# One early product in another bank, and a seventh product ahead of a fourth, in a hybrid attention trunk

## The chip, the cores and the metric

The kernel runs on one core of one Trainium2 chip. The metric is the device time of one execution in microseconds (us). Each profiled execution comes with its own time and with the span of its instructions. The engines are named as in the profile: PE multiplies matrices, PEld loads its weights, DVE and ACT work elementwise (both read what PE left in its accumulators), POOL is a third elementwise engine, and SP issues most of the transfers.

## The reference

One decoder layer over 1024 positions of width 1024 in float32. A normed input is projected to 7184 columns, which feed eight heads of differential softmax attention and four heads of chunked gated linear attention. Both results are normed and gated, and one output projection follows.

```python
h = rms_norm(x, pre_g)
z = jnp.einsum('bsd,de->bse', h, w_in)
qa, ka, va, ga, qb, kb, vb, gb, gk_low = split_columns(z)
...
oa = diff_attention(qa, ka, va, lam)        # softmax(q1 k1) - lam * softmax(q2 k2), times v
gk = jnp.einsum('bsr,re->bse', gk_low, w_gk_up) + b_gk
ob = gla_chunked(qb, kb, vb, log_sigmoid(gk) / 16)
y = jnp.einsum('bse,ed->bsd', jnp.concatenate([oa, ob], axis=-1), w_out)
return x + rms_norm(y, post_g)
```

(Reshapes, norms and gates of the two branches are left out.)

## The kernel before

**The input projection by Strassen's seven products.** For each block of 256 columns, a "pair" p, `w_in` is cut in two halves of rows and two halves of columns, and `h` likewise, and seven products n = 1 to 7 stand for eight. `LEFT` names the block of `h` of each (h11, h12, s1 to s4, h22); each block is kept as a high and a low part, and each product is three passes: high by high, high by low, low by high. Product 1 leaves its sum in a PSUM bank x and a copy s1 of it (`snap`, L427, on ACT); product 6 adds to the same bank and is copied as s2; product 7 adds again and is copied as s3. Product 2 takes a bank y of its own, 5 a bank z, 4 a bank y, and 3 adds to z. Each output quarter (`done`) is the sum, on DVE, of a bank and a copy. For value columns ("VB", "VA") it is L403, for others L440.

**Banks.** There are eight PSUM banks. `take_bank` takes the first number of the list `free`, and whoever is through with a bank appends it. The list is worked in the order in which the program is written; on the chip, a matmul into a bank waits until the last reader of the bank is done.

**The start.** The 1024 rows of x are normed and transposed on PE (`xT`, L120) in two halves. `first(0)` and `first(1)` make h11 and h12. Then `blocks(j)`, j = 0 to 3, each transposes two tiles of the second half into two banks, from which ACT and DVE make h22 and the blocks s1, s2, s3 (L522, L562, L565, L568, L569 and L547/L548). Between these, `go(1)` runs one early product. `step(i)` runs product i of the list `order`; its first ten entries are written out by hand, and the products of the first group (pairs 0 and 1, the first value columns) and of the second (pairs 2 and 3) follow, so that products 5, 6, 4, 7, 3 of the first group come as (0,5) (1,5) (0,6) (1,6) (0,4) (0,7) (1,4) (1,7), with (0,3) (1,3) later. The swap of (1,4) and (0,7) is written out:

```python
i = order.index((1, 4))
order[i : i + 2] = order[i + 1], order[i]
```

With each product, `make_weights` prepares the weights three products ahead: a difference on DVE (L296), a rounded copy on ACT (L315) and the rest on DVE (L316), in a ring of five slots. A wide group (two pairs) uses two slots for a product.

**The low-rank step.** After `go(6)`, `low_rank()` (L630 to L677) loads a 1024 x 16 slice of `w_in` (tile wd) and makes of it a padded matrix wl on DVE (L647, L649 twice, L650 twice) and, of another small input, ku (L653 to L656). It then runs `go(2)`, which is the two last products (1,4) and (1,7) of the first group, and then the product `gkl_ps`, which multiplies by wl.

**After that** come the other pairs, the linear attention, from about 640 us on the scores of the softmax attention (`sc`, in three banks; DVE reads them at L1039, ACT takes the exponential at L1049, POOL and DVE combine the two maps at L1055 and L1058, PE transposes the result, `wtr`), and the output projection.

**Order of work.** PE's order is the program's. The order of DVE, ACT and SP is drawn up at build time by a list scheduler that plans with costs of its own, so a change at one place can reorder these queues at others. Each engine works its queue strictly in order.

Of the kernel before, what the change touches and what calls it, by code (L numbers as in the profile page):

```python
# [19 lines left out]
HB = 4  # L20
# [11 lines left out]
def hymba_kernel(  # L32
# [75 lines left out]
    free = list(range(8))  # L108

    def take_bank(shape, name):  # L110
        i = free.pop(0)
        return bank(i, shape, name), i
# [6 lines left out]
    def tr(dst, src):  # L119
        tc.keep_in_program_order(pe.transpose(dst, src, ident))  # L120
# [11 lines left out]
    def block(n):  # L132
        if n not in H:
            pool_h, pieces = (hpool, 1) if n in ("s3", "s4") else (hw, 2)
            H[n] = [
                [
                    pool_h.tile(
                        [P, HB // pieces, 512], F32R, tag=f"{n}_{part}{i}", name=f"{n}_{part}"
                    )
                    for i in range(pieces)  # L140
                ]
                for part in ("hi", "lo")
            ]
        return H[n]
# [12 lines left out]
    def t2k(tag, bufs, name, dt=F32, shape=(P, 512)):  # L157
        return ap.tile(list(shape), dt, tag=tag, name=name, bufs=bufs)

    def t_c(name, dt=F32):  # L160
        return t2k("c", 4, name, dt)
# [19 lines left out]
    def wide(p):  # L181
        return pairs[p][0] in ("VA", "VB")
# [17 lines left out]
    order = [(0, 1), (1, 1), (0, 2), (1, 2), (2, 1), (3, 1), (2, 2), (3, 2), (4, 1), (4, 2)]  # L200
    n_early = len(order)
    y, z = len(pairs) - 2, len(pairs) - 1
# [12 lines left out]
                order += [(p, 3) for p in prev]  # L215

    i = order.index((1, 4))
    order[i : i + 2] = order[i + 1], order[i]

    order += [(y, 1), (y, 2), (y - 1, 3), (y, 5), (z, 1), (z, 2), (z, 5), (y, 6), (z, 6), (y, 4)]  # L220
    order += [(y, 7), (z, 4), (z, 7), (y, 3), (z, 3)]
# [16 lines left out]
    def prepare(i):  # L238

        if i >= len(order) or i in ws:  # L240
            return
        if i < 4:

            act_ins, dve_ins = normed[0][:2]
            with tc.issue_after(act_ins.ins), tc.issue_after(dve_ins.ins):
                make_weights(i)
        else:
            make_weights(i)
# [73 lines left out]
    def multiply(i, ps, start):  # L322
        p, n = order[i]
        hi, lo = H[LEFT[n]]
        w = ws.pop(i)
        if not wide(p):
            for j, (a, b) in enumerate(((0, hi), (1, hi), (0, lo))):
                for k in range(HB):
                    mm(
                        ps, w[a][:, k, :], at(b, k),  # L330
                        start=(start and j == 0 and k == 0), stop=(j == 2 and k == HB - 1),
                        skip_group_check=not start,
                    )
            return

        for j, (a, b) in enumerate(((0, hi), (1, hi), (0, lo))):
            for k in range(HB):
                for t in range(2):
                    c = (p % 2 * 2 + t) * P
                    mm(  # L340
                        ps[:, t * 256 : t * 256 + 256], at(b, k)[:, c : c + P], w[a][:, k, :],
                        start=(start and j == 0 and k == 0 and t == 0),
                        stop=(j == 2 and k == HB - 1), skip_group_check=True,
                    )
# [51 lines left out]
    def take_values(p, half, unit, p0, p1):  # L396

        kind, n, _ = pairs[p - p % 2]
        tiles = slice(half * 4 + p % 2 * 2, half * 4 + p % 2 * 2 + 2)
        p0, p1 = (t.rearrange("p (n u c) -> p u n c", u=2, c=P) for t in (p0, p1))  # L400
        if kind == "VB":
            st = t_st("gv_st").rearrange("p (u n c) -> p u n c", u=2, c=P)
            dve.tensor_tensor(st, p0, p1, ALU.add)  # L403
            for u in range(2):
                sp.dma_start(gv_d[n + unit][u, :, tiles, :], st[:, u])
        else:
            c, hi = t_c("c"), t_st("v_hi", F32R)
            c, hi, lo = (
                t.rearrange("p (u n c) -> p u n c", u=2, c=P) for t in (c, hi, c.bitcast(F32R))
            )  # L410
            dve.tensor_tensor(c, p0, p1, ALU.add)
            act.copy(hi, c)
            dve.tensor_tensor(lo, c, fp(hi), ALU.subtract)
            for t, src in enumerate((hi, lo)):
                for u in range(2):
                    sp.dma_start(v_d[n + 2 * unit + u][t, :, tiles, :], fp(src[:, u]))
# [3 lines left out]
    def step(i):  # L420

        p, n = order[i]
        kind, m, _ = pairs[p]
        def snap(k, ps):
            other = k == "s3" and (wide(p) or p >= len(pairs) - 2)
            b[k] = t_c("s") if other else t2k("s", 4, "s")
            act.copy(b[k], ps)  # L427

        b = sums.setdefault(p, {})
        name = {1: "x", 2: "y", 5: "z", 6: "x", 4: "y", 7: "x", 3: "z"}[n]  # L430
        if n in (1, 2, 4, 5):
            b[name], b["i" + name] = take_bank([P, 512], name)
        ps = b[name]
        multiply(i, ps, n not in (6, 7, 3))

        def done(half, unit, p0, p1):
            if wide(p):
                return take_values(p, half, unit, p0, p1)
            c = t_c("c")
            dve.tensor_tensor(c, p0, p1, ALU.add)  # L440
            take(kind, m, half, unit, c)

        if n == 1:
            snap("s1", ps)
        elif n == 2:
            done(0, 0, ps, b["s1"])
            free.append(b["iy"])
        elif n == 6:
            snap("s2", ps)
        elif n == 7:  # L450
            snap("s3", ps)
            free.append(b["ix"])
            done(1, 1, b["z"], b["s3"])
            done(1, 0, b["y"], b["s3"])
            free.append(b["iy"])
        elif n == 3:
            done(0, 1, ps, b["s2"])
            free.append(b["iz"])
# [60 lines left out]
    def put(ps, k, dst, j):  # L519
        hi, lo = dst  # L520
        act.activation(at(hi, j), ps, AF.Copy, scale=pre_g[:, k : k + 1])
        dve.scalar_tensor_tensor(  # L522
            at(lo, j), ps, pre_g[:, k : k + 1], fp(at(hi, j)), ALU.mult, ALU.subtract
        )
# [20 lines left out]
    def parts(n, j, f):  # L545
        hi, lo = block(n)
        act.copy(at(hi, j), f)  # L547
        dve.tensor_tensor(at(lo, j), f, fp(at(hi, j)), ALU.subtract)  # L548

    def blocks(j):  # L550


        pss = []
        for k in (j, j + HB):
            ps, i = take_bank([P, 512], "xT")
            for n in range(4):
                tr(ps[:, n * P : (n + 1) * P], xs[4 + n][:, k * P : (k + 1) * P])
            pss.append(ps)
            free.append(i)
        k = j + HB  # L560
        h21 = t_c("h21")
        act.activation(h21, pss[0], AF.Copy, scale=pre_g[:, j : j + 1])  # L562
        put(pss[1], k, block("h22"), j)
        s1 = t_c("s1")
        dve.scalar_tensor_tensor(s1, pss[1], pre_g[:, k : k + 1], h21, ALU.mult, ALU.add)  # L565
        parts("s1", j, s1)
        h11 = f1[0][:, j]
        dve.tensor_tensor(h21, h11, h21, ALU.subtract)  # L568
        dve.tensor_tensor(h11, s1, h11, ALU.subtract)  # L569
        parts("s2", j, h11)  # L570
        parts("s3", j, h21)
# [8 lines left out]
    def wo_step(n):  # L580
        if n in (1, 6) and wo_open:
            e, dh, raw = wo_open.pop()
            hi = t_c("wo_hi", F32R)
            act.copy(hi, raw)
            lo = raw.bitcast(F32R)
            dve.tensor_tensor(lo, raw, fp(hi), ALU.subtract)
            for t, src in enumerate((hi, lo)):
                sp.dma_start(wod[e][t][:, cols(dh)], fp(src))
        if n in (2, 4) and wo_todo:
            e, dh = wo_todo.pop(0)  # L590
            raw = ap.tile([P, 512], F32, tag="t4", name="wo_raw", bufs=1)
            sp.dma_start(raw, w_out[0, e * P : (e + 1) * P, cols(dh)])
            wo_open.append((e, dh, raw))

    def go(n):
        for _ in range(n):
            i = made[0]
            if i == len(order):
                return
            made[0] = i + 1  # L600
            for a in range(4):
                prepare(i + a)
            step(i)
            if order[i][0] > EARLY and not (wide(order[i][0]) and order[i][0] % 2):
                wo_step(order[i][1])
            if fill and next(fill[0], 0) == 0:
                fill.pop(0)
# [10 lines left out]
    go(1)  # L618
    for j in range(HB):
        blocks(j)  # L620
        go(1)
    go(2)
    s4 = [kp.tile([P, 2, 512], F32, tag=f"k{i}", name="s4") for i in range(2)]
# [902 lines left out]
```

## Time and profile before

| | |
|---|---|
| three runs | 980.25, 978.34, 980.24 us; median 980.24 |
| profiled execution | 979.08 us; span of its instructions 977.4 us; TensorE clock granted 0.999 |
| PE busy | 956.7 us (98% of the span) |
| DVE / ACT / POOL busy | 735.4 / 600.5 / 142.9 us |

In a line of the timeline the first number is the start in us from the beginning of the span, the second the duration, then engine, source line, operation, tiles (written <- read), shape and count; square brackets give idle time of the engine just before and what ended it. In a table of waits, a row says which engine's instruction waited for which other: total us, times, longest. In a table of windows a row gives, after the stretch and its length, the busy time of PE, PEld, DVE, ACT and POOL, then the granted clock.

### The profile page before, as it was taken

To read this page: it belongs to the slowest core of one execution; us is meant where nothing else is said; L and a number is where in the kernel's file an instruction comes from. 1 tells how busy PE (TensorE), PEld (TensorE's weight loads), DVE (VectorE), ACT (ScalarE), POOL (GpSimd) and SP (SyncE) were. 2 spreads that over 40 slices of the span, in tenths; PEclk is the share of its full clock that TensorE was granted. 3 is DMA by queue.
4 is the path that set the end of the run, shared out by engine and by line. 5 is a ranking of instruction groups with operands and counts; after the bars stand their busy time and mean duration, and the time that the engine had idled before them with its cause. 6 is when DMAs were issued, how large, how long until landed. Compare 5 with 4: busy or idle time off the path is not lost.

```text
span 977.4 us, 15766 instructions
## 1 busy us (share of the span) xinstructions
PE 956.7 (98%) x5338; PEld 830.4 (85%) x5338; DVE 735.4 (75%) x1452; ACT 600.5 (61%) x1164; POOL 142.9 (15%) x158
## 2 busy tenths in 40 slices
PE   5999999999999999999999999999999999999997
PEld 5998988888889998999888888878888888888785
DVE  6887597789866667686786876487888888898554
ACT  8742455487357455454665775366776687887773
POOL 4300000000000010000200002121322222443321
PEclk9999999999999999999999999999999999999999
DMA  9432446656774868897987866987656669994677
GB/s 345 151 110 91 139 135 205 231 179 225 238 247 162 264 187 286 254 294 229 293 259 243 273 202 191 407 269 272 197 186 228 240 199 344 340 294 105 151 208 147
DMA packets 152593, 220.45 MB, mean 226 GB/s; under 512 B 17104, under 2 KB 83664, under 8 KB 152416
## 3 DMA queue, kind: packets, MB, share of 16 engines
q1 hardware_dynamic: 146176, 203.71, 64.1%
q0 software_dynamic: 6336, 15.73, 7.0%
q8 instruction: 42, 0.69, 0.3%
q14 instruction: 39, 0.32, 0.1%
HBM read 133.93 MB, written 88.60 MB: 228 GB/s over the span
## 4 chain that ended last, share of the span: by engine, by line
PE 95%; DVE 2%; ACT 1%; DMA 1%; issue 1%; POOL 0%; SPq 0%; DVEq 0%; ACTq 0%; POOLq 0%
PE x L117 24%; PE y L117 15%; PE z L117 15%; PE ypart L117 13%; PE sc L117 7%; PE po L117 5%; PE yps L117 4%; PE wtr L120 3%; PE gpo L117 3%; PE kv L117 1%; PE gkl_ps L117 1%; PE pa L117 1%; DMA x<-in_x_dram 1%; PE xT L120 1%; DVE s_lo L548 0%
## 5 line engine op out<-in xcount | busy, mean ns | idle before, releaser
L315 ACT CAST w<-w_raw 128x512 fp32r<-128x512 f32 (+1 forms) x164 | 112.4, 688 | 94.7 <-PE y L117 44.1
L316 DVE TENSOR_TENSOR w<-w_raw,w 128x512 fp32r<-128x512 f32 (+1 forms) x164 | 126.7, 774 | 50.1 <-ACT w L315 43.3
L1049 ACT ACTIVATE p<-p,stt 128x896 f32<-128x896 f32 (+7 forms) x128 | 99.3, 777 | 36.7 <-DVE stt L1039 33.9
L427 ACT COPY s<-x 128x512 f32<-128x512 f32 x84 | 49.1, 585 | 84.4 <-PE x L117 84.3
L775 POOL TENSOR_SCALAR_AFFINE_SELECT gan<-gan 128x512 f32<-128x512 f32 x8 | 16.5, 2060 | 485.4 <-ACT gan L774 449.8
L296 DVE TENSOR_TENSOR w_raw<-w_raw 128x512 f32<-128x512 f32 (+1 forms) x96 | 75.9, 791 | 13.9 <-DMA w_raw<-in_w_in_dram 12.6
L1039 DVE CUSTOM_DVE_ANT_0 p<-sc,maskt 128x512 f32<-128x512 f32 (+3 forms) x128 | 74.3, 585 | 14.5 <-PE sc L117 13.3
L117 PE MATMUL ypart<-wo_hi,m_hi 128*128 128x512 f32 x192 | 79.5, 414 | 0.1
L117 PE MATMUL y<-h_hi,w 128*128 128x512 f32 x320 | 79.6, 391 | 0.0
L117 PE MATMUL z<-s_hi,w 128*128 128x512 f32 x320 | 79.6, 391 | 0.0
L117 PE MATMUL x<-s_hi,w 128*128 128x512 f32 x320 | 79.6, 391 | 0.0
L1055 POOL TENSOR_SCALAR p<-p,stt,lam 128x1024 f32<-128x1024 f32 (+3 forms) x64 | 56.2, 879 | 146.9 <-DVE stt L1054 141.9
L117 PE MATMUL ypart<-wo_hi,m_lo 128*128 128x512 f32 x192 | 75.5, 393 | 0.0
L117 PE MATMUL ypart<-wo_lo,m_hi 128*128 128x512 f32 x192 | 75.4, 393 | 0.0
L117 PE MATMUL sc<-k,q 128*128 128x512 f32 (+1 forms) x192 | 69.0, 363 | 1.3 <-DVE stt L1039 1.2
L117 PEld LDWEIGHTS x<-s_hi,w 128*128 128x128 f32 x320 | 59.7, 188 | 12.2
L117 PEld LDWEIGHTS y<-h_hi,w 128*128 128x128 f32 x320 | 59.6, 188 | 12.2
L117 PEld LDWEIGHTS z<-s_hi,w 128*128 128x128 f32 x320 | 59.5, 188 | 12.0
L117 PE MATMUL sc<-ks,q 128*128 128x512 f32 (+1 forms) x192 | 66.1, 347 | 0.0
L1097 ACT CAST wt_hi<-wtr 128x512 fp32r<-128x512 f32 (+1 forms) x80 | 42.7, 534 | 24.6 <-PE wtr L120 23.8
L1098 DVE TENSOR_TENSOR wt_lo<-wtr,wt_hi 128x512 fp32r<-128x512 f32 (+1 forms) x80 | 50.7, 633 | 8.6 <-ACT wt_hi L1097 8.0
L1058 DVE SCALAR_TENSOR_TENSOR p<-p,stt,p 128x1024 f32<-128x1024 f32 (+3 forms) x64 | 52.1, 814 | 4.1 <-POOL p L1055 3.9
(226 smaller groups left out, 2247.7 us busy)
## 6 DMA issues: line engine op xcount, KB each, us to landing
w_raw<-in_w_in_dram SPq DMA_DIRECT2D x56, 512.0 KB, 4.7
wo_raw<-in_w_out_dram SPq DMA_DIRECT2D x32, 256.0 KB, 3.0
wo_d<-wo_hi SPq DMA_DIRECT2D x32, 256.0 KB, 2.8
wo_d<-wo_raw SPq DMA_DIRECT2D x32, 256.0 KB, 3.8
q<-q_d SPq DMA_DIRECT2D x32, 256.0 KB, 4.7
k<-k_d SPq DMA_DIRECT2D x32, 256.0 KB, 5.7
ks<-k_d SPq DMA_DIRECT2D x64, 128.0 KB, 6.2
v<-v_d SPq DMA_DIRECT2D x16, 512.0 KB, 7.0
```

The costliest lines, as they stand in the source:

```text
L117: tc.keep_in_program_order(pe.matmul(*a, **k))
L120: tc.keep_in_program_order(pe.transpose(dst, src, ident))
L296: dve.tensor_tensor(dst, a, b, ALU.subtract)
L315: act.copy(w[0], src)
L316: dve.tensor_tensor(w[1], src, fp(w[0]), ALU.subtract)
L427: act.copy(b[k], ps)
L1039: ins = dve.tensor_tensor_reduce(p[:, a:e], sc[:, : e - a], maskt[:, NZ + P - (e - a) :] if last else maskt[:, : e - a], 1.0, 3e38 if i == ...
L1049: act.activation(p[:, :n], p[:, :n], AF.Exp, bias=st[:, m : m + 1], scale=-1.0, accum_out=st[:, 2 + m : 3 + m],)
L1055: pool.tensor_scalar(p1[:, :n], p1[:, :n], st[:, 5:6], lam, ALU.mult, ALU.mult)
L1058: dve.scalar_tensor_tensor(p0[:, :n], p0[:, :n], st[:, 4:5], p1[:, :n], ALU.mult, ALU.subtract)
L1097: act.copy(hi[:, :n], pt[:, :n])
L1098: dve.tensor_tensor(lo[:, :n], pt[:, :n], fp(hi[:, :n]), ALU.subtract)
```

## The change

Three edits. First, the order of the first group's second half becomes (0,4) (0,7) (1,7) (1,4): product 7 of pair 1 stands ahead of its product 4. Second, since the quarter `done(1, 0)` needs bank y of product 4 and copy s3 of product 7, it is now run by whichever of the two comes last, and the bank y is given back there. Third, after the last `blocks` and ahead of the product that follows, the second entry of `free` is moved to the front. The list there is [6, 0, 2, 5] and becomes [0, 6, 2, 5]: product 2 of pair 3 takes bank 0 in place of bank 6, and product 1 of pair 4 takes 6 in place of 0. Work and shapes are the same.

```diff
     i = order.index((1, 4))
-    order[i : i + 2] = order[i + 1], order[i]
+    order[i : i + 3] = order[i + 1], order[i + 2], order[i]
...
             done(1, 1, b["z"], b["s3"])
-            done(1, 0, b["y"], b["s3"])
-            free.append(b["iy"])
+        if n in (4, 7):
+            b.setdefault("both", []).append(n)
+            if len(b["both"]) == 2:
+                done(1, 0, b["y"], b["s3"])
+                free.append(b["iy"])
         elif n == 3:
...
     for j in range(HB):
         blocks(j)
+        if j == HB - 1:
+
+            free.insert(0, free.pop(1))
         go(1)
```

## The prediction

> **What bounds the kernel now.** I read the page's first two lines, then PE's own table of waits.
>
> ```profile
> span 977.4 us, 15766 instructions
> PE 956.7 (98%) x5338; PEld 830.4 (85%) x5338; DVE 735.4 (75%) x1452; ACT 600.5 (61%) x1164; POOL 142.9 (15%) x158
> ...
> PE y L117 <- DVE s L565: 1.3, 1, 1.3
> PE sc L117 <- DVE stt L1039: 1.2, 2, 0.9
> PE y L117 <- ACT s L427: 0.7, 1, 0.7
> ```
>
> PE is busy 98% of the span, and after its start-up only some 3 us of waits are named. The change aims at the first and the third of these, 2.0 us together. So every shift of PE that is not taken back later is a shift of the end, and the questions are what PE meets next after each wait that goes, and whether a new wait appears.
>
> **First edit: the bank.** (timeline of PE and DVE, and one row of the windows)
>
> ```profile
> 41.63 1.04 PE L120 MATMUL xT<-ident,xt 128*128 128x128 f32 x8
> 43.98 2.15 PE L117 MATMUL y<-w,h_hi 128*128 128x256 f32 x16 [1.32 <-DVE s L565]
> ...
> 41.83 0.69 DVE L403 TENSOR_TENSOR gv_st<-y,s 128x512 f32<-128x512 f32 x1 [0.16 <-PE y L117]
> ...
> 42.50:62.00 19.50, 18.08 (x128) 16.79 (x127) 19.50 (x29) 10.46 (x16) 0.74 (x1) 1.00 0.21 63
> ...
> 58.09 1.22 DVE L316 TENSOR_TENSOR w<-w_raw,w 128x1024 fp32r<-128x1024 f32 x1
> 58.15 2.44 PE L117 MATMUL x<-w,s_hi 128*128 128x256 f32 x16
> 59.37 1.01 PEld L117 LDWEIGHTS x<-w,s_hi 128*128 128x128 f32 x8 [0.30 <-DVE w L316]
> ```
>
> Before, product 2 of pair 3 waits for L565 to read bank 6. With bank 0 it waits for L403, which reads product 2 of pair 2 there and ends at 41.83 + 0.69 = 42.52. The transposes ahead of it on PE end at 41.63 + 1.04 = 42.67. So it starts at about 42.6 and not at 43.98: 1.35 us gained at this place.
>
> The next product with a late operand is (0,6). Its second eight matmuls need the low weights that L316 writes from 58.09 to 59.31. PE already waited for it there: PEld 59.37 follows its end by 0.06. DVE is busy all of 42.50 to 62.00, 19.50 of 19.50 us. As built, the changed kernel's DVE queue holds the same instructions between L403 at 41.83 and this L316, in a slightly other order; none goes, and none of them waits for a PE product that comes earlier. So L316 ends at 59.31 again, and PE, which reaches it 1.35 us earlier, waits 1.35 us longer. The 1.3 us are not gained but moved; the sum takes 0. (The bounds are 0 and -1.35.) Behind that L316, the changed queue has L363 ahead of the last low part of s2, which is 0.6 us later, at 61.1; PE wants it at 59.4 + 0.96 + 0.72, so 0.1 us at most is lost.
>
> **Second edit: the order.** (timeline of PE, ACT and DVE)
>
> ```profile
> 67.15 2.08 PE L117 MATMUL x<-w,s_hi 128*128 128x256 f32 x16
> 70.87 2.18 PE L117 MATMUL y<-w,h_hi 128*128 128x256 f32 x16 [0.68 <-ACT s L427]
> 73.85 2.08 PE L117 MATMUL x<-w,s_hi 128*128 128x256 f32 x16
> 76.72 2.00 PE L117 MATMUL gkl_ps<-h_hi,wl 128*64 128x512 f32 x8
> ...
> 70.23 0.59 ACT L427 COPY s<-x 128x512 f32<-128x512 f32 x1 [1.62 <-PE x L117]
> ...
> 71.00 0.69 DVE L403 TENSOR_TENSOR gv_st<-z,s 128x512 f32<-128x512 f32 x1
> ...
> 72.20 0.40 DVE L653 CAST ku<-gk_up 16x512 fp32r<-16x512 f32 x1
> ...
> 73.08 0.23 DVE L647 TENSOR_TENSOR wd<-wd 128x64 f32<-128x64 f32 x1
> 73.23 0.22 DVE L649 CAST wl<-wd 128x128 fp32r<-128x128 f32 x1
> 73.48 0.68 DVE L655 TENSOR_TENSOR ku<-gk_up,ku 16x512 fp32r<-16x512 f32 x1
> 74.17 0.68 DVE L656 TENSOR_TENSOR ku<-gk_up,ku 16x512 fp32r<-16x512 f32 x1
> 74.89 1.22 DVE L316 TENSOR_TENSOR w<-w_raw,w 128x1024 fp32r<-128x1024 f32 x1
> 76.03 0.19 DVE L649 CAST wl<-wd 128x64 fp32r<-128x64 f32 x1
> 76.14 0.28 DVE L650 TENSOR_TENSOR wl<-wd,wl 128x128 fp32r<-128x128 f32 x1
> ...
> 77.47 1.22 DVE L296 TENSOR_TENSOR w_raw<-w_raw 128x1024 f32<-128x1024 f32 x1
> ...
> 81.26 1.23 DVE L296 TENSOR_TENSOR w_raw<-w_raw 128x1024 f32<-128x1024 f32 x1 [1.24 <-DMA w_raw<-in_w_in_dram]
> ...
> 86.95 2.08 PE L117 MATMUL z<-w,s_hi 128*128 128x256 f32 x16
> ```
>
> A product takes 76.72 - 73.85 = 2.87 us. (0,7) starts at 67.15 and so ends its issue at 70.02. Before, (1,4) takes the bank that (0,7) filled and waits for the copy at L427 (70.23 to 70.82): it starts at 70.87, 0.85 late. Now (1,7) follows, into its own bank, whose copy is long done. It starts at 70.02, (1,4) at 72.89 with its bank long copied, and PE is free for `gkl_ps` at 75.76: 0.96 us before 76.72. That is the intended gain.
>
> But `gkl_ps` needs wl, whose last part for it is L650 at 76.14 to 76.42, only 0.3 us ahead of PE before. And the changed DVE queue has three instructions newly ahead of this L650, or differently placed. From 71.00 on it reads: L403, L403, L653, L654, then L316 (which stood behind L656), L647, L649, L655, L656, then the L403 of (1,7) and a 1024-wide L296 (both stood behind L650), then L649 and L650. L403 is there because (1,7) now comes earlier. By the rows, start to start: the two L403 72.20 - 71.00 = 1.20; L653 and L654 73.08 - 72.20 = 0.88; L316 76.03 - 74.89 = 1.14; L647 0.15; L649 0.25; L655 0.69; L656 0.72; L403 half of 1.20, so 0.60; L296, as long as L316, 1.14; L649 0.11; L650 to its end 0.28. The sum is 7.16. The queue starts when the copy of (0,7) is done, about 70.9. So wl is ready at 78.06 and PE starts `gkl_ps` at about 78.1 in place of 76.72: **1.4 us lost**, a new PE wait of 2.3 us. Nothing on the way waits longer than its turn: the ring slot of this L316 is free when (1,7) is through its first sixteen matmuls, about 72.1, and its turn comes at 73.0; the copy for the L403 of (1,7) is made by 73.7, and its turn is at 75.8. DVE has no idle there that could absorb the three, and L650's cover before was 0.3 us. A pace two tenths off either way gives 1.2 and 1.6 as ends.
>
> SP's queue is moved too: the stores behind that L403 now stand ahead of one weight load, which also waits for an L316 that DVE reaches some 1.6 us later. The L296 that reads this load (81.26, after a wait of 1.24 for it) then ends near 84.1. Behind it on DVE stands the reader of the first `gkl_ps`, which frees the bank that the product at 86.95, now 88.3, takes: over 3 us of cover, so I cost it at nothing. If that cover were gone, each us of it would be a us of PE.
>
> From 76.72 to 631 us PE has no wait in the table, so the 1.4 us pass on whole: nothing there has slack to lose or to give.
>
> **Far from the edits: the first scores.** The changed queues differ once more, at 643 to 660 us, where the scheduler put DVE's L1058 (128x896) ahead of the second half of L1039, and the 640-wide L1058 behind an L1039. Times here are those of before; all engines are shifted alike.
>
> ```profile
> 643.84 1.11 POOL L1055 TENSOR_SCALAR p<-p,stt,lam 128x896 f32<-128x896 f32 x1 [3.33 <-DVE stt L1054]
> ...
> 644.94 0.48 DVE L1039 CUSTOM_DVE_ANT_0 p<-sc,maskt,stt 128x256 f32<-128x256 f32 x1
> 645.35 1.15 DVE L1058 SCALAR_TENSOR_TENSOR p<-p,stt,p 128x896 f32<-128x896 f32 x1
> 645.49 0.50 PE L117 MATMUL sc<-k,q 128*128 128x512 f32 x1
> ...
> 647.16 0.33 PE L117 MATMUL sc<-k,q 128*128 128x128 f32 x1 [0.94 <-DVE stt L1039]
> ...
> 651.31 0.89 DVE L1058 SCALAR_TENSOR_TENSOR p<-p,stt,p 128x640 f32<-128x640 f32 x1 [0.42 <-POOL p L1055]
> ...
> 652.54 0.60 PE L120 MATMUL wtr<-ident,p 128*128 128x128 f32 x4
> ```
>
> L1058 must wait for POOL, 643.84 + 1.11 = 644.95, so that half of L1039 starts 1.06 later (646.41 - 645.35 before, by L1058's pace), and the product at 645.49, into the bank that it frees, at 646.6: 1.1 late. The wait of 0.94 at 647.16 takes nearly all of this back. But the exponential of that half, and with it POOL and the later L1058, also come about 1 us later; the 640-wide L1058 starts near 652.2 and ends near 653.1, and the transposes at 652.54 that read it start 0.6 late. Nothing later on PE waits. I take **0.6 us**; its ends are 0 (the shift is eaten by the wait at 647.16) and 1.7 (both stalls count in full).
>
> [...] New PE waits of 1.7 us at 57.7 and of 2.3 us at 75.8 could cost more than themselves.
>
> ```profile
> 14.41 4.24 PE L117 MATMUL x<-w,h_hi 128*128 128x256 f32 x16 [0.58 <-ACT h_hi L521]
> 18.45 1.72 PE L117 MATMUL x<-w,h_lo 128*128 128x256 f32 x8
> ...
> 23.67 1.12 PE L117 MATMUL x<-w,h_lo 128*128 128x256 f32 x8
> ```
>
> Eight equal matmuls take 1.72 us at the start and 1.12 a little later: PE starts slow. After the 1.32 us idle at 43.98 there is no such thing (16 in 2.15). [...] No run here shows an idle of 2.3 us.
>
> **Sum.** 0 + 1.4 + 0.6 = +2.0 us. On the profiled execution, 979.08, this gives 981.1; on the median, 980.24, which is 1.2 higher, 982.2. I forecast the middle, 981.7. About 0.2% (2.0 us) is what a measurement of this kernel can tell from no change.
>
> **Rivals.**
> - **Both waits simply go** (faster). If L316 at 58.09 and wl at 76.42 came earlier with PE, the gain is 1.35 + 0.96, less 0.6: 1.7 to 2.3, so about 978. For it: these are the two waits that PE's table names. Against: DVE has no idle from 42.5 to 62 and decides both. It needs DVE to finish 1 us earlier than its rows add up to. 0.08.
> - **Only the wl wait counts**: the stall of the scores is absorbed at 647.16. +1.4, 981.1. The wait of 0.94 speaks for it. 0.07.
> - **The scores cost in full**, 1.7 in place of 0.6: +3.1, 982.8. 0.10.
> - **The clock falls** in the 2.3 us wait. The start's 24 slow matmuls end at 20.17, 5.8 us after 14.41; at the pace of 23.67 they take some 3.1. +2.6 more, 984.3. The 43.98 row speaks against it. 0.05.
>
> **How the numbers follow.** The forecast has 0.70. It lies on the border of 0.2%; since 0.1 us at 61.1 was left out of the sum I put 0.44 of it above and 0.26 within. Slower: 0.44 + 0.10 + 0.05 = 0.59. Same: 0.26 + 0.07 = 0.33. Faster: 0.08. The range runs from 979.7, the wl wait alone on the lowest run (978.34 + 1.4), to 984.0, the full stalls on the median and 0.7 for the scatter of the runs; it leaves out the faster rival and the clock.
>
> **What would show it.** Right: `y` starts at 42.6 with no wait of note, PE waits about 1.7 us for L316 before 59.4, (1,7) follows (0,7) without a gap, and `gkl_ps` starts at 78.1 after some 2.3 us of waiting for L650; near 652 to 655 a short wait of `wtr` for L1058. Wrong: `gkl_ps` before 76.7, or L316 of (0,6) ending before 59, or matmuls at 1.72 per eight behind 78.

## The result, and the profile after

The changed kernel takes **981.74 us** (median of 20 runs, 980.21 to 984.97) beside 979.65 us of the kernel before (median of 20 runs on the same chip, 978.34 to 981.47). The ratio is 1.0025, with a 95% interval of 1.0018 to 1.0032: slower by 1.8 to 3.1 us. Its profiled execution took 980.21 us.

Each execution also comes with the mean of its granted TensorE clock, 1 being full speed. Eleven of the 20, with 0.998 or 0.999, took 980.21 to 981.80 us (median 980.95), and nine, with 0.996 or 0.997, took 982.43 to 984.97 (median 983.03). The profiled one is of the eleven; of the nine no trace was kept.

The page's first lines and PE's table of waits, after (who waited for whom: us in total, times, longest). Lines behind the edits have moved: L316 and L403 are where they were, L650 is now L656, L1039 is L1045, L1058 is L1064.

```profile
span 978.5 us, 15760 instructions
PE 956.5 (98%) x5338; PEld 830.1 (85%) x5338; DVE 735.4 (75%) x1452; ACT 601.2 (61%) x1164; POOL 143.4 (15%) x158
...
PE gkl_ps L117 <- DVE wl L656: 2.2, 1, 2.2
PE x L117 <- DVE w L316: 1.5, 1, 1.5
PE sc L117 <- DVE stt L1045: 1.3, 2, 1.0
...
PE wtr L120 <- DVE p L1064: 0.4, 1, 0.4
```

The engines do the same work as before (956.7 and 735.4 us on PE and DVE there). Both waits at which the change aims are gone. In their place stand two others: 1.5 us for L316 and 2.2 us for wl. A third, of 0.4 us, is 570 us away.

The span alone would mislead. This execution reached the first group 0.90 us earlier than the one of before: the transposes ahead of `y` start at 40.73 and not at 41.63, since the waits for x at the start came to 8.6 us and not 9.4. That belongs to neither kernel, as the profiled executions below scatter there in the same way. So each kernel is read from its own transposes (xT, the last L120 ahead of that `y`). PE and then DVE, after:

```profile
40.73 1.04 PE L120 MATMUL xT<-ident,xt 128*128 128x128 f32 x8
41.67 2.17 PE L117 MATMUL y<-w,h_hi 128*128 128x256 f32 x16
...
58.47 1.22 PE L117 MATMUL x<-w,s_hi 128*128 128x256 f32 x8 [1.49 <-DVE w L316]
...
66.38 2.08 PE L117 MATMUL x<-w,s_hi 128*128 128x256 f32 x16
69.26 2.08 PE L117 MATMUL x<-w,s_hi 128*128 128x256 f32 x16
72.14 2.08 PE L117 MATMUL y<-w,h_hi 128*128 128x256 f32 x16
77.38 2.02 PE L117 MATMUL gkl_ps<-h_hi,wl 128*64 128x512 f32 x8 [2.21 <-DVE wl L656]
...
57.18 1.24 DVE L316 TENSOR_TENSOR w<-w_raw,w 128x1024 fp32r<-128x1024 f32 x1
...
72.17 1.23 DVE L316 TENSOR_TENSOR w<-w_raw,w 128x1024 fp32r<-128x1024 f32 x1
...
75.11 0.69 DVE L403 TENSOR_TENSOR gv_st<-z,s 128x512 f32<-128x512 f32 x1
75.72 1.22 DVE L296 TENSOR_TENSOR w_raw<-w_raw 128x1024 f32<-128x1024 f32 x1
...
76.95 0.29 DVE L656 TENSOR_TENSOR wl<-wd,wl 128x128 fp32r<-128x128 f32 x1
```

`y` follows its transposes without a wait, 0.94 us behind their start; before it was 43.98 - 41.63 = 2.35. So 1.41 us are gained there. L316 still starts 57.18 - 40.73 = 16.45 us behind the transposes, as in before (58.09 - 41.63 = 16.46), and PE waits for it. Then (0,7), (1,7), (1,4) follow one another at 66.38, 69.26 and 72.14 without a gap, and PE stands before `gkl_ps` for 2.21 us, waiting for L656. L316 stood ahead of this instruction in before too; new ahead of it are L403 at 75.11 and L296 at 75.72. From xT to `gkl_ps` it is 36.65 us; before it was 35.09. The 1.56 us are lost to the edits in the first group.

The third loss, in the scores, after (DVE, then PE):

```profile
645.68 1.15 DVE L1064 SCALAR_TENSOR_TENSOR p<-p,stt,p 128x896 f32<-128x896 f32 x1 [0.18 <-POOL p L1061]
646.75 0.48 DVE L1045 CUSTOM_DVE_ANT_0 p<-sc,maskt,stt 128x256 f32<-128x256 f32 x1
...
643.12 0.50 PE L117 MATMUL sc<-k,q 128*128 128x512 f32 x1 [0.29 <-DVE stt L1045]
647.29 0.50 PE L117 MATMUL sc<-k,q 128*128 128x512 f32 x1 [1.04 <-DVE stt L1045]
653.85 0.66 PE L120 MATMUL wtr<-ident,p 128*128 128x128 f32 x4 [0.40 <-DVE p L1064]
```

The 256-wide score part now stands behind the 128x896 weighting, and a 512-wide product waits 1.04 us for the bank that it frees. From the first of these `sc` to `wtr` it is 653.85 - 643.12 = 10.73 us. In before the same `sc` starts at 642.43 and `wtr` at 652.54, 10.11 us apart. That is 0.62 us more. PE's last matmul ends at 971.80; before it ended at 970.69. With the 0.90 us of the start that makes 2.0 us. The loss of the first group, 1.56 at `gkl_ps` and 1.59 at this `sc`, and the 0.62, less some 0.2 that PE catches up near 818 us, make it up. This is a sum over one execution of each kernel.

### The profile page after: what moved, and what is told of

Read it like the earlier page. It is cut to its first block, busy times and chain, and to the rows that moved or that the text cites. A ratio compares the mean times of both kernels' runs of the same rounds, so it can differ in the third digit from the quotient of the medians.

```text
span 978.5 us, 15760 instructions
## 1 busy us (share of the span) xinstructions
PE 956.5 (98%) x5338; PEld 830.1 (85%) x5338; DVE 735.4 (75%) x1452; ACT 601.2 (61%) x1164; POOL 143.4 (15%) x158
## 4 chain that ended last, share of the span: by engine, by line
PE 95%; DVE 2%; issue 1%; DMA 1%; ACT 1%; SPq 0%; POOL 0%; DVEq 0%; ACTq 0%; POOLq 0%
PE x L117 24%; PE z L117 16%; PE y L117 16%; PE ypart L117 13%; PE sc L117 7%; PE po L117 5%; PE yps L117 4%; PE wtr L120 3%; PE gpo L117 3%; PE kv L117 1%; PE gkl_ps L117 1%; DMA w_raw<-in_w_in_dram 1%; PE pa L117 1%; PE xT L120 1%; DVE p L1045 0%
## 5 line engine op out<-in xcount | busy, mean ns | idle before, releaser
L316 DVE TENSOR_TENSOR w<-w_raw,w 128x512 fp32r<-128x512 f32 (+1 forms) x164 | 127.2, 777 | 52.0 <-ACT w L315 45.7
L296 DVE TENSOR_TENSOR w_raw<-w_raw 128x512 f32<-128x512 f32 (+1 forms) x96 | 75.6, 787 | 18.4 <-DMA w_raw<-in_w_in_dram 17.0
L1045 DVE CUSTOM_DVE_ANT_0 p<-sc,maskt 128x512 f32<-128x512 f32 (+3 forms) x128 | 74.3, 585 | 14.1 <-PE sc L117 12.8
L1064 DVE SCALAR_TENSOR_TENSOR p<-p,stt,p 128x1024 f32<-128x1024 f32 (+3 forms) x64 | 52.1, 814 | 4.5 <-POOL p L1061 4.3
```

What stands on the lines that cost most here:

```text
L296: dve.tensor_tensor(dst, a, b, ALU.subtract)
L316: dve.tensor_tensor(w[1], src, fp(w[0]), ALU.subtract)
L1045: ins = dve.tensor_tensor_reduce(p[:, a:e], sc[:, : e - a], maskt[:, NZ + P - (e - a) :] if last else maskt[:, : e - a], 1.0, 3e38 if i == ...
L1064: dve.scalar_tensor_tensor(p0[:, :n], p0[:, :n], st[:, 4:5], p1[:, :n], ALU.mult, ALU.subtract)
```

## The experiments

Ten kernels were run in three lots, each timed in five rounds beside the kernel before on the same chip. Ratios are to that kernel before, with their 95% intervals. "xT to gkl_ps" is the distance described above (35.09 before, 36.65 after), "sc to wtr" the other (10.11 and 10.73).

### e1_bank: the first edit alone

```diff
         blocks(j)
+        if j == HB - 1:
+            free.insert(0, free.pop(1))
         go(1)
```

> The kernel before with the first edit alone: the early y of pair 3 takes the other free bank, the list of products is as it was. Theory (the bank's gain is swallowed): y starts about 1.3 us earlier, at 42.6 on the clock of before's profile, the second eight matmuls of product (0,6) then wait about 1.5 us for the low weights of L316 as in the changed kernel, and the rest of the first group runs as in before; the time is that of before within 0.3 us (ratio 0.9997 to 1.0003). Rival A (the bank edit carries the changed kernel's loss, since the early product delays VectorE's queue): 981.7, about 2 us slower than before. Rival B (the 1.3 us arrive at the end): 978.3, ratio 0.9986.

Measured: 979.67 us, ratio 0.9993 (0.9984 to 1.0001). PE's timeline of this kernel:

```profile
40.90 1.03 PE L120 MATMUL xT<-ident,xt 128*128 128x128 f32 x8
41.84 2.18 PE L117 MATMUL y<-w,h_hi 128*128 128x256 f32 x16
...
58.64 1.22 PE L117 MATMUL x<-w,s_hi 128*128 128x256 f32 x8 [1.48 <-DVE w L316]
...
76.11 2.00 PE L117 MATMUL gkl_ps<-h_hi,wl 128*64 128x512 f32 x8
```

`y` starts 1.41 us earlier against its transposes, the wait of 1.48 us stands at (0,6), and xT to `gkl_ps` is 35.21, 0.12 more than before. The ratio lies a little under the expected band (0.9997 to 1.0003), and its interval reaches into it. Rival A is out: its ratio, 1.0020, lies outside the interval. The time alone doesn't exclude rival B, but the trace does: of 1.41 us nothing is left at `gkl_ps`.

### e2_order: the second edit alone

The changed kernel without the edit of e1:

```diff
     i = order.index((1, 4))
-    order[i : i + 2] = order[i + 1], order[i]
+    order[i : i + 3] = order[i + 1], order[i + 2], order[i]
...
+        if n in (4, 7):
+            b.setdefault("both", []).append(n)
+            if len(b["both"]) == 2:
+                done(1, 0, b["y"], b["s3"])
+                free.append(b["iy"])
```

> The changed kernel without its first edit: only the products of the second half change places and their result is combined after the later of the two. Theory (the loss is in this edit): gkl_ps waits about 2.2 us for the low-rank weights wl as in the changed kernel, the scores at about 645 us run in the changed kernel's order, and the time is the changed kernel's, about 2 us above before (ratio 1.0020, 1.0015 to 1.0025). Rival A (the loss needs the bank edit): the time of before, ratio 1.0000. Rival B (both edits lose one half each): ratio 1.0010.

Measured: 981.75 us, ratio 1.0020 (1.0011 to 1.0030). Its xT starts at 40.22 and `gkl_ps` at 76.78 after 2.24 us of waiting for wl: 36.56. In the scores it has the waits of the changed kernel (1.04 before `sc`, 0.40 before `wtr`). So the loss belongs to this edit, and the bank edit adds no more than some 0.1 us to it.

### e5_after_wl: the low-rank weights on GpSimd

```diff
-        dve.tensor_tensor(wd, wl[:, HB:], wl[:, :HB], ALU.subtract)
+        pool.tensor_tensor(wd, wl[:, HB:], wl[:, :HB], ALU.subtract)
         for dst, src in ((wl2[:, :KT], wl), (wl2[:, KT:], wd)):
-            dve.tensor_copy(dst[:, :, :R], src)
-            dve.tensor_tensor(dst[:, :, 32 : 32 + R], src, ...)
+            pool.tensor_copy(dst[:, :, :R], src)
+            pool.tensor_tensor(dst[:, :, 32 : 32 + R], src, ...)
```

> The changed kernel with the five small operations that make the low-rank weights wl2 (the difference, two copies, two subtractions) moved from VectorE to GpSimd, so that they don't stand behind the conversions of weights in VectorE's queue. Theory (what holds gkl_ps up is VectorE's queue ahead of wl, not the data): wl is there well before 75.9, the wait of 2.2 us at gkl_ps goes, and the 0.85 us that the order saves at product (1,7) reach the rest; the queue of the scores is built as in before, so their 0.6 us go too; 978.8 us, ratio to before 0.9991 (0.9986 to 0.9998). Rival A (wl waits for its DMA or for the matmuls' banks): gkl_ps starts no earlier and the time stays within 0.3 us of the changed kernel's. Rival B (GpSimd needs over 2 us more for the five than VectorE's 0.1 to 0.4 us each): the wait stays at 1 us or more, 980 us.

Measured: 979.02 us, ratio 0.9993 (0.9984 to 1.0002). POOL and PE in its timeline:

```profile
68.48 0.97 POOL L653 TENSOR_TENSOR wd<-wd 128x64 f32<-128x64 f32 x1 [26.43 <-DMA wd<-in_w_in_dram]
69.41 0.47 POOL L655 CAST wl<-wd 128x128 fp32r<-128x128 f32 x2
69.84 0.73 POOL L656 TENSOR_TENSOR wl<-wd,wl 128x128 fp32r<-128x128 f32 x2
...
40.43 1.04 PE L120 MATMUL xT<-ident,xt 128*128 128x128 f32 x8
74.72 1.99 PE L117 MATMUL gkl_ps<-h_hi,wl 128*64 128x512 f32 x8
```

wl is ready at 70.57, over 4 us ahead of PE, the wait is gone, and xT to `gkl_ps` is 34.29: 2.36 us less than in the changed kernel and 0.80 less than in before. So the 2.2 us came from wl's place in DVE's queue, not from its data, and the reordering of the products does bring its 0.8 us once wl is out of that queue. The scores' queue was built in before's order here, so what separates the ratios of this kernel and the changed one, 0.9993 and 1.0025, isn't this wait's alone.

### e8_after_pin and e9_before_pin: the order of the scores alone

e8 is the changed kernel, with DVE's weighting of query block 6 of head 0 queued behind the score part that it overtook. e9 is the kernel before, with the same two the other way round. `tc.issue_after(i)` queues what is issued under it behind instruction i. Below, e8's edit is called the pin.

```diff
+                    def weights(...):                     # e8: L1064
+                        dve.scalar_tensor_tensor(p0[:, :n], p0[:, :n], st[:, 4:5], p1[:, :n], ...)
+                    if (h, qb) == (0, 6):
+                        late.append(weights)
...
+                if last and m and late:                   # e8: behind L1045 of block 5
+                    with tc.issue_after(ins.ins):
+                        late.pop()()
```

```diff
+                    if (h, qb) == (0, 6):                 # e9: out is the instruction of L1058
+                        lowest.append(out.ins)
...
+                if (h, qb, m) == (0, 5, 1) and last:
+                    behind = tc.issue_after(lowest[1])
```

> The changed kernel with one edge more in VectorE's queue: in head 0 the weighting of query block 6 (L1064, 128x896) is queued behind the last score part of query block 5, which puts the queue of the scores between 641 and 656 us back into before's order; the first group is the changed kernel's. Theory (0.6 us of the 2.0 are lost in the scores through the order alone): the start of wtr is again about 10.1 us behind the score matmuls' start at 642.43 of before, and the time is 0.6 us (0.4 to 0.8) under the changed kernel's, ratio to before 1.0014. Rival (the scores absorb it, and what is lost there is noise of one execution): the changed kernel's time, ratio 1.0021 or more.

> The kernel before, its first group untouched, with one edge more in VectorE's queue: in head 0 the second score part (256 wide) of query block 5 is queued behind the weighting of query block 6 (128x896), which gives the scores between 641 and 656 us the changed kernel's order. Theory (the order alone costs the far 0.6 us): sc at 645.49 of before starts about 1.1 us later, wtr at 652.54 about 0.6 us later, and the time is 0.6 us (0.4 to 0.8) above before, ratio 1.0006. Rival (the delay in the changed kernel came with its later first group, not with the order): no step at 645 us, ratio 1.0000.

Measured: e8 980.50 us, ratio 1.0007 (0.9996 to 1.0018); e9 980.40 us, ratio 1.0010 (1.0001 to 1.0019). PE in the scores, e8 first:

```profile
645.02 0.50 PE L117 MATMUL sc<-k,q 128*128 128x512 f32 x1 [0.29 <-DVE stt L1045]
649.76 0.33 PE L117 MATMUL sc<-k,q 128*128 128x128 f32 x1 [0.95 <-DVE stt L1045]
655.14 0.60 PE L120 MATMUL wtr<-ident,p 128*128 128x128 f32 x4
```

```profile
643.32 0.50 PE L117 MATMUL sc<-k,q 128*128 128x512 f32 x1 [0.29 <-DVE stt L1041]
647.49 0.50 PE L117 MATMUL sc<-k,q 128*128 128x512 f32 x1 [1.04 <-DVE stt L1041]
654.03 0.66 PE L120 MATMUL wtr<-ident,p 128*128 128x128 f32 x4 [0.40 <-DVE p L1060]
```

sc to wtr is 10.12 in e8, before's 10.11, though its first group is the changed kernel's (xT 40.51, `gkl_ps` 77.18, 36.67). It is 10.71 in e9, the changed kernel's 10.73, though its first group is before's. So in the traces the order of these two instructions is the whole of the 0.6 us. The times agree in sign, but their intervals are wider than what is looked for: that an average execution changes by 0.6 us they don't show.

### e11_bank_pool_pin: the bank, with s4 on GpSimd

Before with the bank edit, the pin of e8, and

```diff
-        dve.tensor_tensor(s4[j // 2][:, j % 2], f1[1][:, j], f1[0][:, j], ALU.subtract)
+        pool.tensor_tensor(s4[j // 2][:, j % 2], f1[1][:, j], f1[0][:, j], ALU.subtract)
```

> The kernel before with the first edit (the other bank) and with the four differences s4 (L625, 128x512) computed on GpSimd instead of VectorE; the order of products is as before, and the scores' queue is held in before's order by the edge of e8. Theory (the bank's 1.4 us are lost because VectorE has no slack up to the low weights of (0,6); four operations of about 0.65 us less there make it): the wait of 1.5 us at (0,6) goes, gkl_ps starts about 1.7 us earlier against the transposes just before y, and the time is 1.7 us (1.0 to 2.0) under before, ratio 0.9983. Rival A (the low weights wait for their DMA): the wait stays, ratio 0.9995 to 1.0000. Rival B (GpSimd is too slow for s4 or slows VectorE beside it, so that (1,4) and (1,7) wait for s4): slower than before, ratio 1.0005 or more.

Measured: 983.12 us, ratio 1.0035 (1.0021 to 1.0049): the expectation was wrong. POOL, DVE and PE in its timeline:

```profile
50.34 6.32 POOL L628 TENSOR_TENSOR s<-f1lo,f1hi 128x512 f32<-128x512 f32 x2 [5.49 <-DVE f1hi L569]
54.32 1.19 DVE L548 TENSOR_TENSOR s_lo<-f1hi,s_hi 128x512 fp32r<-128x512 f32 x1
55.44 1.77 DVE L548 TENSOR_TENSOR s_lo<-h,s_hi 128x512 fp32r<-128x512 f32 x1
...
59.53 1.22 PE L117 MATMUL x<-w,s_hi 128*128 128x256 f32 x8 [3.01 <-DVE w L316]
```

Of the two rivals this is B in its second half: GpSimd slows DVE beside it. The subtraction that takes 0.69 us elsewhere takes 1.19 and 1.77 here, and the two on POOL take 6.32 us together where the pair before them, at 41.86, took 3.00 and slowed two L548 to 1.31 and 1.78. The four L548 take 6.05 us in place of 4 x 0.69 = 2.76, so 3.29 us are lost, where the three s4 that left DVE ahead of L316 save 3 x 0.6 = 1.8. So L316 comes 1.5 us later than in before and PE waits 3.0 us for it. xT to `gkl_ps` is 36.61. In six of its nine executions the mean clock is 0.997 or less, so the clock may have a share in the median. The loss in the first group is a price of GpSimd, and says nothing yet on whether s4 is what swallows the bank's gain; e13 asks that.

### e10_best_pin and e6_best: everything at once, on GpSimd

e10 is the changed kernel with the edits of e5, e8 and e11 as they are shown above; e6 is e10 without that of e8.

> Both edits of the changed kernel, with the low-rank weights wl2 and the differences s4 on GpSimd and the scores' queue in before's order: all three covers that were found missing are put back. Theory: the 1.4 us of the bank and the 0.85 us of the order both arrive, with 0.3 us more from the emptier VectorE; gkl_ps starts about 2.5 us earlier than in before, and the time is 2.5 us (1.7 to 3.0) under it, ratio 0.9974. Rival (the gains don't add, since GpSimd then holds one of the two up): gkl_ps 0.8 to 1.7 us earlier, ratio 0.9983 to 0.9992.

> e10 without the edge in the scores' queue, which the scheduler then builds anew: the weighting of query block 6 (128x896) stands ahead of both score parts of query block 5, one place earlier still than in the changed kernel. Theory: a first group as in e10 (2.5 us gained), and in the scores some 1.5 us lost, by the replay of before's durations in that order; 1.0 us under before, ratio 0.9990. Rival (the scores absorb the order): the time of e10.

Measured: e10 981.78 us, ratio 1.0017 (1.0006 to 1.0028); e6 984.01 us, ratio 1.0048 (1.0032 to 1.0064). Both have the late L316 of e11, and something more. First PE and a row of the windows (behind POOL's busy time stands the granted clock, a mean over the stretch) in e10, then the same in e6:

```profile
59.77 2.08 PE L117 MATMUL x<-w,s_hi 128*128 128x256 f32 x8 [3.01 <-DVE w L316]
61.65 1.54 PE L117 MATMUL x<-w,s_lo 128*128 128x256 f32 x8
...
60.00:64.00 4.00, 4.00 (x25) 4.00 (x26) 4.00 (x7) 3.34 (x6) 0.00 (x0) 0.67 0.73 198
```

```profile
59.52 2.08 PE L117 MATMUL x<-w,s_hi 128*128 128x256 f32 x8 [2.99 <-DVE w L316]
61.40 1.91 PE L117 MATMUL x<-w,s_lo 128*128 128x256 f32 x8
63.10 3.10 PE L117 MATMUL x<-w,s_hi 128*128 128x256 f32 x16
...
60.00:64.00 4.00, 4.00 (x21) 4.00 (x21) 4.00 (x7) 3.08 (x6) 0.00 (x0) 0.50 0.71 198
...
652.00:656.00 4.00, 4.00 (x12) 3.09 (x12) 3.00 (x10) 1.85 (x5) 1.12 (x2) 0.57 1.02 268
```

After 3 us of idle the eight matmuls that take 1.22 us in e11 take 2.08, at a granted clock of 0.67 and 0.50. These are means over 4 us. If the clock stands at 0.50 throughout, as in e6 from 60 to 64 us, the means from 56 to 68 us (0.90, 0.67, 1.00 in e10; 0.83, 0.50, 0.82 in e6) make that an estimated 3.4 us in e10 and 6.8 us in e6. Up to the product behind it, that costs 63.03 - 59.77 = 3.26 us in e10, where e11 needs 2.02. In e6 it lasts one product longer, 7.48 us up to 67.00 where e11 needs 4.90: 2.6 us. The unpinned scores of e6 have a wait of 1.42 us and then the low clock once more: sc to wtr is 13.18, 3.1 more than before, where 1.5 was expected. So neither theory nor rival was right in its numbers, of e10 or of e6.

### e13_bank_s4late: the bank, with s4 on DVE but later

Before with the bank edit, the pin of e8, and s4 made two products later (its old place goes; `low06` holds the L316 of product (0,4)):

```diff
-    go(6)
+    go(2)
+    s4 = [...]
+    for j in range(HB):
+        with tc.issue_after(low06[0]):        # L316 of product (0,4)
+            dve.tensor_tensor(s4[j // 2][:, j % 2], f1[1][:, j], f1[0][:, j], ALU.subtract)
...
+    go(4)
```

> The kernel before with the first edit (the other bank), the four differences s4 still on VectorE, but queued there behind the low weights of product (0,4) instead of ahead of those of (0,6), since their first product comes at about 80 us; the scores' queue is held in before's order as in e8. Theory after e11 (the bank's gain is lost to what stands ahead of L316 in VectorE's queue, and e11 failed since GpSimd's subtractions slowed VectorE beside them): the three s4 ahead of L316 go, 1.8 us, the wait of 1.5 us at (0,6) with them, gkl_ps starts about 1.4 to 1.7 us earlier against the transposes ahead of y, and the time is 1.5 us (0.8 to 1.8) under before, ratio 0.9985. Rival A (the low weights of (0,6) wait for their DMA or for ScalarE's copy, whatever stands ahead): the wait stays at 1 us or more, ratio 0.9995 to 1.0000. Rival B (s4 comes too late for its copies on ScalarE and its product): gkl_ps or the z behind it waits, ratio 1.0005 or more.

Measured: 978.74 us, ratio 0.9993 (0.9984 to 1.0003). xT at 40.35, then no wait at (0,6), `gkl_ps` at 73.83: 33.48, 1.61 less than before. So it was the place of s4 in DVE's queue that swallowed the bank's gain; that part of the theory holds. The time fell short: about 0.7 us in place of 1.5, with an interval that takes in both. The profiled execution shows where gains can go: PE and DVE near 410 us,

```profile
409.59 0.49 PE L117 MATMUL gpo<-gqd,gu 128*128 128x128 f32 x2 [1.69 <-DVE gu L810]
...
407.92 1.23 DVE L296 TENSOR_TENSOR w_raw<-w_raw 128x1024 f32<-128x1024 f32 x1 [2.39 <-DMA w_raw<-in_w_in_dram]
```

where DVE stands 2.39 us for a weight load, gu is queued behind it, and PE waits 1.69 us for gu. The executions of before and after that were profiled have no PE wait there; those of the other experiments have one of 0.3 to 1.2 us, one execution each. With this wait and others, at 364 us and between 500 and 550, PE loses 0.8 to 3.0 us against before between 100 and 640 us in every one of the ten profiled executions of the experiments; the changed kernel's loses nothing there. Whether the load comes when it comes or follows PE, and how much of an early gain it takes on the average, stays open.

### e12_all: all three covers put back

The changed kernel with the edits of e13 (s4 late), e5 (wl on GpSimd) and e8 (the pin) as they are shown above.

> The changed kernel with all three covers put back and no large operation on GpSimd: s4 queued on VectorE behind the low weights of (0,4) as in e13, the low-rank weights wl2 on GpSimd as in e5, the scores' queue in before's order as in e8. Theory: the bank's 1.4 us and the order's 0.85 us both arrive, with some 0.2 us more; gkl_ps starts about 2.5 us earlier than in before and nothing on TensorE waits there; the time is 2.5 us (1.5 to 3.0) under before, ratio 0.9975, and about 4.5 us under the changed kernel. Rival (one of the two gains is taken by the next wait, as at the low weights of (0,4) or at a free ring buffer): gkl_ps 0.8 to 1.7 us earlier, ratio 0.9983 to 0.9992.

Measured: **976.62 us, ratio 0.9973 (0.9962 to 0.9985)**. It beats both kernels. Its PE:

```profile
41.03 1.03 PE L120 MATMUL xT<-ident,xt 128*128 128x128 f32 x8
41.98 2.17 PE L117 MATMUL y<-w,h_hi 128*128 128x256 f32 x16
...
73.44 1.99 PE L117 MATMUL gkl_ps<-h_hi,wl 128*64 128x512 f32 x8
```

xT to `gkl_ps` is 32.41, 2.68 less than before, with no PE wait between the two. In this execution 0.8 us went to the wait for gu near 410 us, and at the last matmul 1.9 us of the 2.68 are left.

| kernel | xT to gkl_ps | sc to wtr | ratio (95%) |
|---|---|---|---|
| before | 35.09 | 10.11 | 1 |
| changed | 36.65 | 10.73 | 1.0025 (1.0018 to 1.0032) |
| e1, bank | 35.21 | | 0.9993 (0.9984 to 1.0001) |
| e2, order | 36.56 | | 1.0020 (1.0011 to 1.0030) |
| e5, wl on GpSimd | 34.29 | | 0.9993 (0.9984 to 1.0002) |
| e8 / e9, pins | 36.67 / 35.08 | 10.12 / 10.71 | 1.0007 (0.9996 to 1.0018) / 1.0010 (1.0001 to 1.0019) |
| e11 | 36.61 | | 1.0035 (1.0021 to 1.0049) |
| e10 / e6 | 36.91 / 38.25 | - / 13.18 | 1.0017 (1.0006 to 1.0028) / 1.0048 (1.0032 to 1.0064) |
| e13 | 33.48 | | 0.9993 (0.9984 to 1.0003) |
| e12 | 32.41 | | 0.9973 (0.9962 to 0.9985) |

## Why the prediction was right, point by point

- **The bank brings 1.35 and leaves 0.** Right, with 1.41 gained at `y` and 1.49 waited at (0,6). L316 came 16.45 us behind the transposes, as in before, to 0.01. e1 alone shows 0.12 us of loss; e13 shows that the gain arrives once DVE has less to do ahead of L316. The low parts behind it took 0.14 us longer (1.26 for 1.12, PE's timeline), where 0.1 was allowed.
- **The order gains 0.96 and loses 1.4 at wl.** Right in kind, 0.16 short in size. (1,7) and (1,4) followed without a gap. DVE needed 77.24 - 70.08 = 7.16 us from its first L403 to the end of L656, the very sum of the rows. PE started 0.14 us behind that end, and the queue began 0.08 later than taken (70.98 on before's clock). e2 and e5 show that this is the edit's whole loss in the first group. What moves in SP's queue, costed at nothing, did cost nothing: the L296 that reads the later weight load ended at 83.89 (84.79 on before's clock, where 84.1 was forecast), the reader behind it was through at 84.47, and PE took its bank at 87.62 without a wait.
- **The 1.4 us pass on whole from there to 631 us.** Right for this pair of executions: the shift was 1.56 at 77 us and is 1.59 at 643. As a rule it is too strong: the wait for gu alone takes up to 1.7 us in other executions. Nor do the times bear it out: the eleven executions at 0.998 or 0.999 have a median 1.3 us above before (980.95 and 979.65), where the traces add up to 2.0, and in e8, whose first group loses the same 1.6 us, the eight executions at these clocks have one 0.2 us above (980.24 and 980.05). How much of the shift an average execution keeps stays open.
- **The scores, 0.6.** Right in the trace: 0.62, by the mechanism named. e8 takes it away and e9 makes it, each with the other kernel's first group.
- **The clock, costed at nothing.** Right in the profiled executions, and most likely wrong beyond them. That waits of 1.7 and 2.3 us leave the clock alone was the author's estimate: before shows it for 1.32 us of idle only. In the traces a wait of 2.2 us leaves the clock alone: `gkl_ps` takes 2.02 for eight behind it, 2.00 before, e2 and e8 are alike, and the granted clock is 1.00 from 78 to 82 us in these three kernels. But a mean clock of 0.997 or less, and with it some 2 us more, is on record for 14 of the 42 executions of the three kernels with this wait (9 of 20 of the changed one, 2 of 11 of e2, 3 of 11 of e8). Of the kernels whose traces show neither this wait nor one of 3 us it is on record for 2 of 128 (before in the three lots, e1, e5, e9, e12, e13), and of the three with a wait of 3.0 us for 22 of 27 (e11, e10, e6). e5, the changed kernel without the wait for wl, has none among its 11. So the rival that was given 0.05 seems to have come true in nearly half of the changed kernel's executions, with 2.1 us between the medians of the two groups where it named 2.6. Its 2.6 came from the slow matmuls of the start, and that the clock makes these slow is not shown: in before the granted clock is 1.00 there too (14 to 20 us). That the clock falls behind this very wait is inferred from which kernels show it; no trace of such an execution exists. At 3.0 us of idle the traces show the fall in two of three executions, in e6 at the price that the rival named, 2.6 us.
- **The sum, and its base.** Here luck has a share. +2.0 was forecast for the waits and the scores, and the profiled executions show 2.0 once the start is taken out. The medians differ by 2.09, but that is a mixture: 1.3 us in the eleven executions, 3.4 in the nine of the lower clock. In the eleven the waits and the scores gave less than the 2.0 forecast, and the clock, which the sum put at nothing, made up for it in the median. The base was a choice too: 979.08 or 980.24 could be taken, from one and from three runs. The median of twenty runs, 979.65, happens to lie at their middle, so 981.7 met 981.74 closer than its working deserved.
- **Both waits simply go.** Wrong for this change, and the three reasons against it are the three edits of e12, which does get there.

## What to carry to other kernels

Here a wait that a bank or an order took away on TensorE was a gain only where the next operand's producer had slack (in e1 1.41 us were gained at `y` and 1.48 waited at (0,6); in e13, with s4 later, 1.61 arrived at `gkl_ps`). So read what stands ahead of that producer in its engine's queue, and move what isn't needed yet (s4, wl) behind it or elsewhere together with the edit. Where a scheduler draws up the queues, compare the whole of them, since a swap of two instructions 570 us away cost 0.6 of the 2 us in the trace. To judge differences of this size, measure from a landmark ahead of the edit: the start alone moved the profiled executions by up to 1.4 us. And look at the granted clock of every execution, not of the profiled one alone: here it parts the times of the changed kernel into two groups 2 us apart.

## What the runs showed of the hardware that was not expected

**Subtractions on GpSimd and VectorE beside one another took longer.** A 128x512 subtraction of two float32 tiles takes VectorE 0.69 us alone, and the four L548 in e11 that ran beside the same on GpSimd took 1.19 to 1.78. GpSimd's own four took 3.00 us for the two from 41.86 on and 6.32 for the two from 50.34 on. Beside these last, five of VectorE's operations (50.78 to 53.72) kept their usual times, 0.68 or 0.69 us and 1.22 for L296, before two L548 took 1.19 and 1.77. The rows don't show what decides which of the two engines takes longer, nor what GpSimd needs for such a subtraction while VectorE stands. Beside the small operations of e5 (0.97 us for one, 0.47 and 0.73 for two each) the first group lost nothing that shows: xT to `gkl_ps` is 34.29, 0.80 less than before.

**The clock fell behind idle times of 3 us.** Idle times of 2.99 us in e6 and 3.01 in e10 brought it to 0.50 and 0.67, as means over 4 us, in two of three profiled executions (e11, with 3.01, kept 1.00). Idle times of 2.2 us left it at 1.00 in the three that were profiled (the changed kernel, e2, e8), but the mean clocks of all 42 executions of their kernels suggest that it fell in some third of them (14). In e6 even a wait of 1.42 us, in a stretch in which PE was busy 2.38 of 4 us, was followed by 0.57:

```profile
648.00:652.00 4.00, 2.38 (x11) 1.43 (x11) 3.23 (x10) 1.80 (x4) 0.45 (x1) 1.00 0.98 379
```

How long or how often PE must be idle for it was not measured.
